# adaLN products and sums of squares in four 32-column tiles, and the residual's gate moved to the first group's head

## The chip, the cores and the metric

One core of a Trainium2 chip. The time is the device time of one execution in microseconds; of the kernel before there are three: 1978.23, 1971.2 and 1976.4, median 1976.4. Besides, one execution was taken by the hardware profiler; its span is 1971.9 us at a mean granted TensorE clock of 0.990. All durations of single instructions come from that execution.

## The reference

The kernel computes one layer of a bidirectional encoder for two requests ("groups" below: prompt and sample) that share all weights, each of 1024 tokens with 1024 channels, in float32. What the change touches is the frame around the two attention branches:

```
mod = silu(c) @ w_ada + b_ada                   # w_ada: 1024 x 3072, one c for each group
shift, scale, gate = split(mod, 3)
h = rms_norm(x, norm_g) * (1 + scale) + shift
proj = h @ w_in                                 # all of: qa, ka, va, za, qb, kb, vb, zb, ga, gb
oa = gqa_attention(qa, ka, va) * silu(za)       # branch A: 8 heads, RMS-normed, rotated
ob = headwise_norm(diff_attention(...)) * silu(zb)   # branch B
merged = sigmoid(ga) * (oa @ w_proj_a) + sigmoid(gb) * (ob @ w_proj_b)
y = x + gate * (merged @ w_out)
```

So `shift` and `scale` are needed before the first projection, while `gate` is needed only in the residual addition at the end of each group.

## The kernel before, in words

**Data.** Activations are kept transposed: channels on the 128 partitions, tokens along the free dimension, eight chunks of 128 channels, two halves of 512 tokens. For the large products each operand is split into a high and a low part in a rounded fp32 type, and a product is three matmuls (high x high, high x low, low x high). Weights come in pieces of 256 KB into small staging tiles ("st", three of them), from where ACT (L179) and POOL or DVE (L181) split them into a weight tile ("w", two of them). Large tiles ("u", 15 of 8 KB per partition) hold the activations, and in the head also the adaLN weights. PSUM has two large tiles ("s"), three of one bank ("f") and one for the attention's values ("a"). While no attention runs, `gbank()` deals out both s and f.

**Order.** The program text says which work belongs between which: `weave()` takes steps of several generators in turn, by shares. A scheduler then orders the instructions on each engine, with the attention's scores first; each engine works through its list in order and waits on semaphores. All DMAs that the change touches are issued by SP, one list, in order: a DMA that waits for its buffer holds up those behind it.

**The head of the first group.** `start()` (L339) loads c, the first half of x and eight 1 MB pieces of w_ada (L245 to L250: two column halves of shift and of scale, each in two row halves). `ada()` (L294) multiplies SiLU(c), 128 channels x 2 groups, as the stationary operand with 512 columns of w_ada: 4 chunks per piece, all added up in one PSUM row pair over 8 chunks (L300). These are plain fp32 products, which the trace shows as two passes each. `ada_end()` (L302) copies the 2 x 512 sums to SBUF (L306), transposes them by four small products (L309) and adds the bias (L313). For the RMS norm, ACT squares x (L256); for the first half of the tokens `added()` (L259) adds the eight chunks on DVE (L262 to L265) and `inv_rms()` (L268) sums over partitions by 128x1 products with a column of ones (L273), POOL takes the power -1/2 (L280), `spread()` (L283) brings the result to all partitions by products with the identity (L287) and an ACT copy (L289), and DVE and POOL multiply x by it (L356). For the second half there is no addition on DVE: `inv_rms()` gets all eight chunks, 32 products of 128x1 (64 passes). The shift and scale of that half stand in `start_late()` (L368), which `head()` (L1018) calls after the first six steps of the k/v projection of branch A and three of z: spread, then x times scale times statistics (L374, eight on DVE), shift and high part on ACT (L377, L378), low part on DVE (L379).

**Projections.** `proj_tt()` (matmuls at L514) makes q, k and v, a 128-token tile at a time; `z_gen()` (L692, matmuls at L703) makes the gate paths' inputs, which ACT evicts (L709) and SP stores in DRAM (L712).

**Attention.** 128 scores of branch A and 128 of branch B, half of each in the first group; a score is 128 query rows by 1024 keys for one head. For each: four matmuls (L734, L735), maximum on DVE (L736, L737), exponential on ACT (L738), a transposition on DVE (L771) and further by DMAs, split in two halves (L784 on ACT, L785 on DVE), and the matmuls with the values (L796, L797 for A, L836 for B). Between the scores PE runs "fill": the projections that the next stage needs. In the last stage of each group's attention the fill is made by `fill()` (L1141): z, gates' products and the merge.

**The residual's gate.** `gate_gen()` (L445) is the first thing in that fill of the first group. It loads the last third of w_ada in 16 pieces of 256 KB into the staging tiles (L451), multiplies each as above (L452, 32 passes), copies, transposes (L456, L459) and adds the bias.

Of the kernel before, what the change touches and what calls it, by code (L numbers as in the profile page):

```python
# [20 lines left out]
P = 128  # L21
T = 1024
D = 1024
# [45 lines left out]
WHOLE = (True, True)  # L69

# [20 lines left out]
def kernel(ctx: ExitStack, tc: tile.TileContext, t: dict):  # L91
# [81 lines left out]
    nc.vector.memset(nhalf, -0.5)  # L173

# [57 lines left out]
    cT = const.tile([P, NCH, 2], F32, name="cT")  # L232
# [26 lines left out]
    def added(sq):  # L259

        a, b = sq
        nc.vector.tensor_tensor(out=a[:, :2], in0=a[:, :2], in1=b[:, :2], op=ALU.add)  # L262
        nc.vector.tensor_tensor(out=a[:, 2:], in0=a[:, 2:], in1=b[:, 2:], op=ALU.add)
        nc.vector.tensor_tensor(out=a[:, :2], in0=a[:, :2], in1=a[:, 2:], op=ALU.add)
        nc.vector.tensor_tensor(out=a[:, 0], in0=a[:, 0], in1=a[:, 1], op=ALU.add)  # L265
        return [a[:, 0]]

    def inv_rms(sq):  # L268

        ps = gbank()  # L270
        for k in range(4):
            for i, x in enumerate(sq):
                nc.tensor.matmul(  # L273
                    ps[:, k : k + 1], x[:, k * P : (k + 1) * P], ones_c, start=(i == 0), stop=(i == len(sq) - 1)
                )
# [3 lines left out]
        nc.gpsimd.tensor_scalar(out=ss, in0=ss, scalar1=1.0 / D, scalar2=EPS, op0=ALU.mult, op1=ALU.add)  # L279
        nc.gpsimd.tensor_tensor(out=rs, in0=ss, in1=nhalf[:, :4], op=ALU.pow)  # L280
        return rs
# [12 lines left out]
    def ada(n, wt):  # L294
        hf, third, q = n // 4, n // 2 % 2, n % 2
        if q == 0:
            accs[n // 2] = gbank()[:2]
        acc = accs[n // 2]
        for c in range(4):
            nc.tensor.matmul(acc, cT[:, q * 4 + c], wt[:, c], start=(q == 0 and c == 0), stop=(q == 1 and c == 3))  # L300

    def ada_end(n):  # L302
        hf, third = n // 4, n // 2 % 2
        acc = accs[n // 2]
        row = halves2(ptile())[0][:2]
        nc.vector.tensor_copy(row, acc)  # L306
        ps = gbank()[:, :8].rearrange("p (c g) -> p c g", g=2)
        for c in range(4):
            nc.tensor.transpose(ps[:, c, :], row[:, c * P : (c + 1) * P], ident[:2, :2])  # L309
        cs = slice(hf * 4, hf * 4 + 4)  # L310
        mc = modc[:, third, cs, :]
        both = [P, 4, 2]
# [3 lines left out]
        if third:  # L316
            nc.vector.tensor_tensor(out=mc, in0=mc, in1=gcol[:, cs].unsqueeze(2).to_broadcast(both), op=ALU.mult)
# [21 lines left out]
    def start(ht):  # L339
        nc.scalar.activation(cT, ccol, AF.Silu)  # L340
# [9 lines left out]
        for n in range(8):  # L350
            ada(n, wts[n])
            if n == 3:
                rsb = spread(inv_rms(added(squares(xT[0]))))
# [3 lines left out]
            if n in (2, 4, 6, 7):  # L357
                ada_end(n if n == 7 else n - 1)
            if n == 4:
# [83 lines left out]


    def gate_gen():  # L445
        for half in range(2):
            acc = gbank()[:2]
            for k in range(NCH):
                st = spool.tile([P, 512], F32, tag="st", name=nm("st"))
                col = 2 * D + half * 512  # L450
                dma(st, w_ada[k * P : (k + 1) * P, col : col + 512])  # L451
                nc.tensor.matmul(acc, cT[:, k], st, start=(k == 0), stop=(k == NCH - 1))  # L452
                if k % 2:
                    yield 1
            row = rtile()[:2]
            nc.vector.tensor_copy(row, acc)  # L456
            ps = gbank()[:, :8].rearrange("p (c g) -> p c g", g=2)
            for c in range(4):
                nc.tensor.transpose(ps[:, c, :], row[:, c * P : (c + 1) * P], ident[:2, :2])  # L459
            cs = slice(half * 4, half * 4 + 4)  # L460
            nc.vector.tensor_tensor(
                out=gatec[:, cs], in0=ps, in1=bcol[:, 2, cs].unsqueeze(2).to_broadcast([P, 4, 2]), op=ALU.add
            )
# [554 lines left out]
    def head(g, st, zs, late):  # L1018
# [80 lines left out]
    states = [new_state(0), new_state(1)]  # L1099
    late = start(states[0]["ht"])  # L1100
    load_tables()
    for g in range(2):
# [38 lines left out]
        def fill():  # L1141
            if g == 0:
                yield from gate_gen()
# [68 lines left out]
```

## Time and profile before

| | us |
|---|---|
| times of three executions | 1978.23, 1971.2, 1976.4 |
| span of the profiled execution | 1971.9 |
| PE busy / DVE busy / ACT busy / POOL busy | 1901.8 / 1353.0 / 1012.0 / 680.9 |
| first product of the projections (L514) starts | 42.41 |
| second half's statistics spread (L287) | 66.09 |
| first product of a score (L734) starts | 140.7 |
| products of the residual's gate (L452) | 751.1 to 785.9 |

The profiled execution's own time stands by its span of 1971.9; it lies 4.5 below the median and within the three executions. In a row of the profile, "L703 PE MATMUL f<-u,w 128*128 128x512 f32 x2184 | 561.3, 395" means: 2184 instructions of line 703 on PE that write tile f from tiles u and w, 561.3 us of busy time, 395 ns for the mean one. Records of neighbouring matmuls overlap, so that the pace of a row of matmuls is read from the starts of two groups, not from the mean. "idle before" is the time that the engine stood just ahead of such instructions, and the name behind "<-" is what released it. One instruction of the program's text can stand as two in the trace: a plain fp32 matmul has two passes.

### The profile page before, as it was taken

The page shows a single profiled execution, that of the slowest core. Times are in us where ns is not written, and L with a number is a line of the kernel's source. Part 1 is how long each engine was busy: PE and PEld are TensorE (multiplying, and loading weights), DVE is VectorE, ACT ScalarE, POOL GpSimd, SP SyncE. Part 2 cuts the span into 40 slices and gives each one's busy share as a digit, 9 for nine tenths or more (in the row PEclk, how much of TensorE's full clock was granted, in tenths as well). Part 3 has the DMA queues.
Part 4 walks back from the last instruction along what each step waited for, and adds up shares of the span by engine and source line. Part 5 has one row for each costly group of instructions (what it writes and reads, how often), then busy time and mean ns, then how long its engine had stood idle before and what let it go on. Part 6 is the DMA issues. An engine that isn't in the chain of part 4 may idle for free. (4 is left out here: it accounts for less than half of the span.)

```text
span 1971.9 us, 30870 instructions
## 1 busy us (share of the span) xinstructions
PE 1901.8 (96%) x10466; PEld 1619.1 (82%) x10466; DVE 1353.0 (69%) x2165; ACT 1012.0 (51%) x1920; POOL 680.9 (35%) x958
## 2 busy tenths in 40 slices
PE   8999999999989999999999999999999999998999
PEld 3888888888878985778889788888888889776887
DVE  4658876786888577757465598768878766776641
ACT  4447655565655353464323576556666444447410
POOL 2363511442446251322235344114444426322210
PEclk9899999999999999999999999999999999999999
DMA  9125545556454345865641355555555334478431
GB/s 315 33 89 149 144 139 149 158 156 174 127 144 111 89 117 173 272 234 179 222 151 44 115 144 167 148 149 157 156 152 161 98 102 119 120 222 267 166 102 75
DMA packets 271614, 295.26 MB, mean 150 GB/s; under 512 B 37856, under 2 KB 220256, under 8 KB 271456
## 3 DMA queue, kind: packets, MB, share of 16 engines
q1 hardware_dynamic: 271456, 293.28, 50.1%
q8 instruction: 84, 1.38, 0.3%
q14 instruction: 74, 0.61, 0.1%
HBM read 133.72 MB, written 42.01 MB: 89 GB/s over the span
## 5 line engine op out<-in xcount | busy, mean ns | idle before, releaser
L703 PE MATMUL f<-u,w 128*128 128x512 f32 x2184 | 561.3, 395 | 3.0 <-ACT w L179 1.3
L514 PE MATMUL f<-w,u 128*128 128x256 f32 x3456 | 489.6, 286 | 5.2 <-ACT ev L709 2.7
L514 PEld LDWEIGHTS f<-w,u 128*128 128x128 f32 x3456 | 460.7, 192 | 26.8 <-ACT ev L709 3.7
L703 PEld LDWEIGHTS f<-u,w 128*128 128x128 f32 x2184 | 396.8, 189 | 78.1 <-ACT w L179 1.8
L181 POOL TENSOR_TENSOR w<-st,w 128x512 fp32r<-128x512 f32 x166 | 227.8, 1391 | 463.2 <-ACT w L179 412.9
L736 DVE TENSOR_REDUCE m<-s 128x1 f32<-128x1024 f32 x256 | 310.2, 1217 | 55.1 <-PE s L735 52.0
L771 DVE STREAM_TRANSPOSE p<-p 128x1024 f32<-128x1024 f32 x192 | 238.0, 1241 | 112.8 <-ACT p L738 110.2
L785 DVE TENSOR_TENSOR q<-q,hi 128x512 fp32r<-128x512 f32 x256 | 193.9, 774 | 47.9 <-ACT hi L784 46.4
L738 ACT ACTIVATE p<-s,m,rsB 128x1024 f32<-128x1024 f32 x128 | 154.0, 1204 | 135.0 <-DVE m L737 103.3
L738 ACT ACTIVATE p<-s,m,rsA 128x1024 f32<-128x1024 f32 x128 | 153.8, 1202 | 128.1 <-DMA q<-p 95.8
L735 PE MATMUL s<-u,sw 128*128 128x512 f32 x512 | 205.0, 401 | 0.0
L784 ACT ACTIVATE hi<-q 128x512 fp32r<-128x512 f32 x256 | 153.2, 624 | 78.2 <-DMA q<-p 50.2
L179 ACT ACTIVATE w<-st 128x512 fp32r<-128x512 f32 x196 | 114.2, 626 | 101.9 <-DMA st<-in_w_in_dram 46.6
L976 PE MATMUL f<-u,w 128*128 128x512 f32 x552 | 136.4, 400 | 11.3 <-ACT ev L709 4.1
L796 PE MATMUL a<-hi,u 128*128 128x256 f32 x512 | 132.0, 284 | 4.8 <-DVE oo L813 3.1
L976 PEld LDWEIGHTS f<-u,w 128*128 128x128 f32 x552 | 104.8, 192 | 35.3 <-DVE u L987 4.6
L836 PE MATMUL a<-q,u 128*128 128x256 f32 x512 | 125.9, 385 | 5.6 <-DMA q<-p 1.9
L797 PE MATMUL a<-q,u 128*128 128x256 f32 x512 | 129.8, 287 | 0.5 <-DVE q L785 0.4
L734 PE MATMUL s<-u 128*128 128x512 f32 x256 | 109.5, 428 | 7.9 <-ACT p L738 4.0
L734 PE MATMUL s<-u,u 128*128 128x512 f32 x256 | 103.3, 404 | 13.8 <-ACT p L738 9.0
L836 PEld LDWEIGHTS a<-q,u 128*128 128x128 f32 x512 | 95.9, 193 | 21.6 <-issue 2.9
L735 PEld LDWEIGHTS s<-u,sw 128*128 128x128 f32 x512 | 97.4, 190 | 15.5
(186 smaller groups left out, 2639.1 us busy)
## 6 DMA issues: line engine op xcount, KB each, us to landing
q<-p SPq DMA_DIRECT2D x768, 128.0 KB, 2.6
st<-in_w_in_dram SPq DMA_DIRECT2D x132, 256.0 KB, 3.0
zd<-ev SPq DMA_DIRECT2D x96, 256.0 KB, 2.2
sw<-u SPq DMA_DIRECT2D x256, 64.0 KB, 2.0
p<-zd SPq DMA_DIRECT2D x64, 256.0 KB, 3.8
u<-in_w_ada_dram SPq DMA_DIRECT2D x8, 1024.0 KB, 10.4
st<-in_w_in_dram SPq DMA_DIRECT2D x64, 128.0 KB, 2.7
st<-in_w_out_dram SPq DMA_DIRECT2D x32, 256.0 KB, 3.2
```

The lines of the kernel that those rows point to most:

```text
L181: e.tensor_tensor(out=wl, in0=st, in1=wh.bitcast(F32), op=ALU.subtract)
L514: nc.tensor.matmul(ps, lt[c][:, sl], w[:, c, wi, :], start=(k == 0), stop=(k == 23))
L703: nc.tensor.matmul(ps, w[:, c, wi, e * P : (e + 1) * P], rt[c], start=(k == 0), stop=(k == 23),)
L734: nc.tensor.matmul(s[:, sl], q, k[:, sl], start=True, stop=False)
L735: nc.tensor.matmul(s[:, sl], sw, k[:, sl], start=False, stop=True)
L736: nc.vector.tensor_reduce(out=m, in_=s, axis=AX.X, op=ALU.max, negate=True)
L738: nc.scalar.activation(pt.rearrange("p (j c a) -> p j c a", j=4, c=8), s.rearrange("p (c a j) -> p j c a", c=8, j=4), AF.Exp, scale=rs, bi ...
L771: nc.vector.transpose(pt, pt)
L784: nc.scalar.activation(th, tl.bitcast(F32), AF.Copy)
L785: nc.vector.tensor_tensor(out=tl, in0=tl.bitcast(F32), in1=th.bitcast(F32), op=ALU.subtract)
L836: nc.tensor.matmul(acc, u["v"][:, k], pT[:, k], start=(k == 0), stop=(k == 7))
L976: nc.tensor.matmul(ps, w[:, c, wi, d * P : (d + 1) * P], o[:, oi, :], start=(k == 0), stop=(k == 11))
```

## The change

- **Four products at once in 32-column tiles.** SiLU(c) is kept with 32 columns per chunk, 30 of them zero (`at`). `ada()` gives each of the four chunks of a piece its own 32 partitions of the PSUM bank (`quarter()`), that is, its own column tile of the array; a tile adds up two products only. `ada_end()` copies the whole 128 x 512 bank and contracts the four quarters by products with a 128 x 2 matrix (`two`), which takes the place of the transposes.
- **Sums of squares likewise.** `inv_rms()` multiplies 32 columns of -0.5 with the eight chunks of squares, four tiles with two products each, copies the bank, and contracts it by four 128x1 products; the factor -1/(16 D) makes up for the 32 equal rows and the -0.5. `added()` is gone.
- **Order in the head.** The pieces of w_ada come in the order shift, scale of the first column half, then of the second as before; the first half's statistics are made after the second piece, not the fourth; each pair of pieces is ended at once.
- **The residual's gate** is made in the first group's head by `gates_of_residual()`, right behind `late()`: four loads of 1 MB into u tiles, 16 products in tiles, two `ada_end()`. `gate_gen()` is gone, and with it its place in `fill()`.

```
+ADA = [(third, hf, q) for hf in range(2) for third in range(2) for q in range(2)]
+ADA += [(2, hf, q) for hf in range(2) for q in range(2)]
...
+    two = const.tile([P, 2], F32, name="two")
+    nc.vector.tensor_reduce(
+        out=two, in_=ident.rearrange("p (j r) -> p r j", j=4)[:, :2, :], axis=AX.X, op=ALU.add
+    )
...
-    def added(sq):
...
+    def quarter(ps, c):
+        return ps[32 * c : 32 * c + 32]
 
     def inv_rms(sq):
+        acc = gbank()
+        for i in range(2):
+            for c in range(4):
+                nc.tensor.matmul(quarter(acc, c), nhalf, sq[i][:, c], start=(i == 0), stop=(i == 1))
+        part = rtile()
+        nc.vector.tensor_copy(part, acc)
         ps = gbank()
         for k in range(4):
-            for i, x in enumerate(sq):
-                nc.tensor.matmul(
-                    ps[:, k : k + 1], x[:, k * P : (k + 1) * P], ones_c, start=(i == 0), stop=(i == len(sq) - 1)
-                )
+            nc.tensor.matmul(ps[:, k : k + 1], part[:, k * P : (k + 1) * P], ones_c, start=True, stop=True)
...
     def ada(n, wt):
-        hf, third, q = n // 4, n // 2 % 2, n % 2
+        third, hf, q = ADA[n]
         if q == 0:
-            accs[n // 2] = gbank()[:2]
-        acc = accs[n // 2]
+            accs[third, hf] = gbank()
+        acc = accs[third, hf]
         for c in range(4):
-            nc.tensor.matmul(acc, cT[:, q * 4 + c], wt[:, c], start=(q == 0 and c == 0), stop=(q == 1 and c == 3))
+            nc.tensor.matmul(quarter(acc, c), cT[:, q * 4 + c], wt[:, c], start=(q == 0), stop=(q == 1))
 
     def ada_end(n):
-        hf, third = n // 4, n // 2 % 2
-        acc = accs[n // 2]
-        row = halves2(ptile())[0][:2]
-        nc.vector.tensor_copy(row, acc)
+        third, hf, q = ADA[n]
+        row = rtile()
+        nc.vector.tensor_copy(row, accs[third, hf])
         ps = gbank()[:, :8].rearrange("p (c g) -> p c g", g=2)
         for c in range(4):
-            nc.tensor.transpose(ps[:, c, :], row[:, c * P : (c + 1) * P], ident[:2, :2])
+            nc.tensor.matmul(ps[:, c, :], row[:, c * P : (c + 1) * P], two, start=True, stop=True)
         cs = slice(hf * 4, hf * 4 + 4)
-        mc = modc[:, third, cs, :]
+        mc = modc[:, third, cs, :] if third < 2 else gatec[:, cs, :]
...
     def start(ht):
-        nc.scalar.activation(cT, ccol, AF.Silu)
+        nc.gpsimd.memset(cT, 0.0)
+        nc.scalar.activation(cT[:, :, :2], ccol, AF.Silu)
...
         for n in range(8):
             ada(n, wts[n])
-            if n == 3:
-                rsb = spread(inv_rms(added(squares(xT[0]))))
+            if n == 1:
+                rsb = spread(inv_rms(squares(xT[0])))
...
-            if n in (2, 4, 6, 7):
-                ada_end(n if n == 7 else n - 1)
-            if n == 4:
+            if n % 2:
+                ada_end(n)
+            if n == 3:
                 split_early(kva_w[0])
                 add_h(ht, 0, 0)
                 modulated(ht, 0, xT[0], range(4))
...
-        rs = inv_rms([q[:, c] for q in squares(xT[1]) for c in range(4)])
+        rs = inv_rms(squares(xT[1]))
...
+    def gates_of_residual():
+        for n in range(8, 12):
+            ada(n, load_ada(n))
+            if n % 2:
+                ada_end(n)
...
-    def gate_gen():
...
                 if i == 0:
                     late()
+                    gates_of_residual()
...
+    cT = mtile("at", [P, 256], bufs=1).rearrange("p (c m) -> p c m", c=NCH)
     late = start(states[0]["ht"])
...
         def fill():
-            if g == 0:
-                yield from gate_gen()
             yield from zs
```

In the kernel after, the lines that the prediction names have other numbers: the products of `ada()` stand at L304 (L300 before), the contraction at L312 (L309), the copy of the sums at L309 (L306), the products over the squares at L274 and L279 (L273), the spread at L291 (L287), the second half's L374 and L379 at L384 and L389.

More of the change, by code (lines that the diff above doesn't have):

```diff
@@ L231 @@
     gcol = const.tile([P, NCH], F32, name="gcol")
-    cT = const.tile([P, NCH, 2], F32, name="cT")
     modc = const.tile([P, 2, NCH, 2], F32, name="modc")
@@ L257, in squares @@
         return sq
-    def added(sq):
[L261 to L266, printed above, removed]
-    def inv_rms(sq):
+    def quarter(ps, c):
+        return ps[32 * c : 32 * c + 32]
+    def inv_rms(sq):
+        acc = gbank()
[4 more added lines that the diff above has]
+        nc.vector.tensor_copy(part, acc)
         ps = gbank()
         for k in range(4):
-            for i, x in enumerate(sq):
-                nc.tensor.matmul(
-                    ps[:, k : k + 1], x[:, k * P : (k + 1) * P], ones_c, start=(i == 0), stop=(i == len(sq) - 1)
-                )
+            nc.tensor.matmul(ps[:, k : k + 1], part[:, k * P : (k + 1) * P], ones_c, start=True, stop=True)
         ss = tiny.tile([P, 4], F32, tag="ss", name=nm("ss"))
@@ L278, in inv_rms @@
         nc.vector.tensor_copy(ss, ps[:, :4])
-        nc.gpsimd.tensor_scalar(out=ss, in0=ss, scalar1=1.0 / D, scalar2=EPS, op0=ALU.mult, op1=ALU.add)
+        nc.gpsimd.tensor_scalar(out=ss, in0=ss, scalar1=-1.0 / (16 * D), scalar2=EPS, op0=ALU.mult, op1=ALU.add)
         nc.gpsimd.tensor_tensor(out=rs, in0=ss, in1=nhalf[:, :4], op=ALU.pow)
@@ L294, in ada @@
     def ada(n, wt):
[L295 removed]
+        third, hf, q = ADA[n]
         if q == 0:
[L297 to L298 removed]
+            accs[third, hf] = gbank()
+        acc = accs[third, hf]
         for c in range(4):
[L300 removed]
+            nc.tensor.matmul(quarter(acc, c), cT[:, q * 4 + c], wt[:, c], start=(q == 0), stop=(q == 1))
     def ada_end(n):
[L303 to L306 removed]
+        third, hf, q = ADA[n]
+        row = rtile()
+        nc.vector.tensor_copy(row, accs[third, hf])
         ps = gbank()[:, :8].rearrange("p (c g) -> p c g", g=2)
         for c in range(4):
[L309 removed]
+            nc.tensor.matmul(ps[:, c, :], row[:, c * P : (c + 1) * P], two, start=True, stop=True)
         cs = slice(hf * 4, hf * 4 + 4)
[L311 removed]
+        mc = modc[:, third, cs, :] if third < 2 else gatec[:, cs, :]
         both = [P, 4, 2]
@@ L315, in ada_end @@
         )
-        if third:
+        if third == 1:
             nc.vector.tensor_tensor(out=mc, in0=mc, in1=gcol[:, cs].unsqueeze(2).to_broadcast(both), op=ALU.mult)
@@ L442, in load_tables_A @@
             st[name] = tab
-    def gate_gen():
[L446 to L463, printed above, removed]
     def ht_gen(g, ht):
```

## The prediction

> **What bounds the kernel now.** I read the page's busy table first, then its chain, then the busy time by stretches around the two places that the change touches: the head of the first group (0 to 80 us) and the last stage of its attention (740 to 860 us). Columns of the stretches: length, then busy time and count of PE, PEld, DVE, ACT and POOL, then granted clock, DMA share and GB/s.
>
> ```profile
> span 1971.9 us, 30870 instructions
> PE 1901.8 (96%) x10466; PEld 1619.1 (82%) x10466; DVE 1353.0 (69%) x2165; ACT 1012.0 (51%) x1920; POOL 680.9 (35%) x958
> PE 27%; DVE 5%; DMA 4%; SPq 3%; issue 2%; ACT 2%; POOL 1%; ACTq 0%; DVEq 0%; POOLq 0%
> ```
> ```profile
> 0.00:20.00 20.00, 12.42 (x26) 2.39 (x27) 4.85 (x9) 6.09 (x10) 0.69 (x6) 1.00 0.92 339
> 20.00:40.00 20.00, 20.00 (x59) 5.01 (x57) 12.18 (x20) 8.89 (x15) 7.15 (x6) 1.00 1.08 389
> 40.00:60.00 20.00, 20.00 (x110) 18.55 (x109) 10.25 (x28) 9.48 (x17) 4.94 (x4) 0.67 0.43 100
> 740.00:860.00 120.00, 110.29 (x462) 78.36 (x461) 84.78 (x130) 58.95 (x94) 27.68 (x36) 0.99 0.77 245
> ```
>
> PE is busy 96% of the span and leads the chain, so PE work taken out of a stage in which PE is the limit comes off the time, and PE work put where PE waits costs nothing. Two stretches are special. Up to 40 us the DMA engines are full (shares 0.92 and 1.08): PE looks busy there, but it works through the adaLN products as the weights land. From 40 to 60 us PE is busy throughout at a granted clock of 0.67 only. In the gate's stage PE idles 9.7 of 120 us.
>
> **The change part by part.** *The gate's products leave the attention.* The first fence below is the group of the gate's products and what PE waited for ahead of them; the second shows what eight products cost in a row.
>
> ```profile
> L452 PE MATMUL f<-st,cT x32: 591/592/592, 751.1 to 785.9; 128*2 128x512 f32 x32
>   DMA st<-in_w_ada_dram: 6.7, 10
>   issue: 4.3, 13
> ```
> ```profile
> 22.27 3.60 PE L300 MATMUL s<-u,cT 128*2 128x512 f32 x8
> 25.70 3.60 PE L300 MATMUL f<-u,cT 128*2 128x512 f32 x8
> ```
>
> The second group starts 3.43 us after the first, so one pass costs 0.43 us (a 592 ns record overlaps the next). 32 passes are 13.8 us. To that come the eight transposes (about 0.8) and some 2.5 of the 6.7 us in which PE's queues stood waiting for the gate's 256 KB loads. PE is 92% busy in this stage with the rest of its idle time small, so I count all of it: **-17**, between -13 (the bare passes less a little) and -21 (with all the load waits).
>
> *The head: what goes.* The head's timeline of before:
>
> ```profile
> 37.95 4.25 ACT L256 ACTIVATE q<-u 128x512 f32<-128x512 f32 x8
> 42.41 2.31 PE L514 MATMUL f<-w,u 128*128 128x256 f32 x12
> 40.87 1.28 PE L273 MATMUL f<-ones_c,q 128*128 128x1 f32 x10
> 47.23 8.09 PE L273 MATMUL f<-ones_c,q 128*128 128x1 f32 x50
> 55.18 4.19 PE L703 MATMUL s<-u,w 128*128 128x512 f32 x9
> 66.09 0.60 PE L287 MATMUL f<-ident,rs 128*128 128x128 f32 x4
> 67.54 13.26 SPq L712 DMA_DIRECT2D zd<-ev  x2
> 69.61 0.60 ACT L289 ACTIVATE ev<-f 128x512 f32<-128x512 f32 x1 [1.57 <-PE f L514]
> 70.25 5.93 DVE L374 SCALAR_TENSOR_TENSOR u<-u,modc,ev 128x512 f32<-128x512 f32 x8 [1.68 <-ACT ev L289]
> 61.09 2.23 PE L703 MATMUL s<-u,w 128*128 128x512 f32 x9
> 66.44 3.11 PE L514 MATMUL f<-w,u 128*128 128x256 f32 x24
> ```
> ```profile
> L379 DVE TENSOR_TENSOR u<-u,u x8: 676/679/693, 76.5 to 83.7; 128x512 fp32r<-128x512 f32 x8
> u<-in_w_ada_dram SPq DMA_DIRECT2D x8, 1024.0 KB, 10.4
> ```
>
> The first half's statistics come about 8 us sooner (no four DVE additions, and the spread no longer stands behind two more adaLN products), but that buys nothing: the first product of the input projection (42.41) follows the last adaLN weights and the second half of x, which the full DMA queues deliver no sooner. I expect it at 42.5 to 43 again. The 64 adaLN passes hide behind those loads at any spacing up to today's.
>
> What does count is the second half's sum of squares. Its 64 128x1 products (10 in 1.28 us, 50 in 8.09, four more) cost about 10 us between 40.9 and 55. In their place stand 8 products with 32 columns and four with one. One after another the 8 are 16 passes of 0.43 us, 6.9; four at once 1.7; but they can start as the squares finish (37.95 + 4.25), ahead of the projection. No row of before shows two column tiles at work: today's 32-column tile is always the first. I take a factor of 2 over one after another, because each of these fp32 products runs as two passes in order on one tile, so a neighbour can overlap only part. That gives 3.4 us, mostly behind the squares, and the spread of the second half at about 57 instead of 66.1: **-9**.
>
> *The head: what comes in.* In the built program's PE order, behind that spread, come the first two gate products, then the four contractions with the [128, 2] matrix, and only then the next products of z. Those contractions wait for a DVE copy of the gate's sums, and that copy stands on DVE behind all eight L374 and all eight L379 (the after's L384 and L389). From the rows these are 5.93 + 8 x 0.68 = 11.4 us of DVE work that starts about 1.6 us after the spread: until about 70.5. The first gate weights are late as well: on SP they stand behind the first z eviction, which in turn needs a finished z unit (about 58); at a landing of 10.4 us they arrive between 63 and 69. So from 57.6 to about 70.5 PE has only those gate products, where before it ran 72 products of z and of the k/v projection: **+13** of stall, gate products 8 and 9 in it. If the copy gets through sooner, say when the loads land at 65, it is +8. Gate products 10 and 11 follow among z products, 16 passes at the halved cost less what their weights' landing hides: **+2** (+0.5 to +7). Head: -9 + 13 + 2 = **+6**, from +1 to +13. In the built order the first attention score also stands behind 24 more z products (24 x 0.23 = 5.4 us); they are missing later, so this moves the first score without costing time.
>
> *The order of the first attention stage.* With the gate's pieces gone from the fill, the fill is dealt out otherwise. For nine scores of branch A (the 37th to the 45th) the built program has almost no projection products between the scores: 0.7 us, by the spacings above, where before has 35; by the 96th score the two have done the same sum again. The reason in the order is SP: the fourth piece of the next branch-B weight stands behind the transfers of later scores. Before, in that stretch and up to the 96th score:
>
> ```profile
> 337.00:389.00 52.00, 49.99 (x301) 43.94 (x300) 37.27 (x57) 32.31 (x63) 22.00 (x31) 1.00 0.57 160
> 389.00:660.00 271.00, 264.59 (x1555) 233.53 (x1554) 209.77 (x327) 152.67 (x305) 114.35 (x192) 0.99 0.50 139
> L736 DVE TENSOR_REDUCE m<-s x8: 1186/1216/1225, 345.2 to 385.3; 128x1 f32<-128x1024 f32 x8
> L785 DVE TENSOR_TENSOR q<-q,hi 128x512 fp32r<-128x512 f32 x17 | 12.2, 726 | 7.1 <-ACT hi L784 7.0
> L771 DVE STREAM_TRANSPOSE p<-p 128x1024 f32<-128x1024 f32 x9 | 11.2, 1242 | 7.0 <-ACT p L738 7.0
> L737 DVE TENSOR_TENSOR m<-m,rsA 128x1 f32<-128x1 f32 x8 | 1.4, 177 | 0.3
> L813 DVE TENSOR_TENSOR oo<-a,at 64x256 f32<-64x256 f32 x4 | 1.7, 418 | 0.1
> ```
>
> A score's own PE work is four products at 0.23 and eight at 0.13: 2.0 us. Its DVE work is 1.22 + 1.24 + 2 x 0.73 + 0.18 + 0.2 = 4.3, and with a little slack I take 4.5 us per score when nothing fills PE. Nine such scores leave PE idle 9 x 2.5 = 22.5 us. Before, PE idled 8.4 us in all from 337 to 660 us (2.0 and 6.4). The put-off 34 us of fill can take up nearly all the later idle time, not more. So 22.5 - 8.4 = 14, less about 1 for slack that other stretches give: **+13**. Bounds: the fastest pace of scores without much fill that before shows is branch B's in the second group,
>
> ```profile
> 1516.00:1544.00 28.00, 25.54 (x131) 20.85 (x130) 21.56 (x33) 12.82 (x25) 8.27 (x12) 1.00 0.57 157
> L736 DVE TENSOR_REDUCE m<-s x7: 1186/1217/1225, 1519.2 to 1542.6; 128x1 f32<-128x1024 f32 x7
> ```
>
> 6 steps in 23.4 us, 3.9 each; less some fill, 3.6. At 3.6 it is 9 x 1.6 - 8.4 = +6; at 5.2 (the chain with its transfers not overlapped) 9 x 3.2 - 8.4 = +20.
>
> *The second group.* Its order shifts by a few products only (up to 12 us of fill earlier, level again at score 192): **+2**, from -2 to +7, as the nearest stretch with idle PE there has 4.5 us of it:
>
> ```profile
> 1100.00:1140.00 40.00, 35.53 (x185) 29.65 (x184) 22.55 (x32) 26.66 (x42) 7.98 (x9) 0.96 0.46 126
> ```
>
> **Sum**: -17 + 6 + 13 + 2 = +4 on the span, 1971.9 to 1975.9. The profiled span is 4.5 below the median of 1976.4, so the median becomes about 1980.
>
> **The skill beside it.** The Trainium skill, "TensorEngine Tiling (Array Packing)", section Theoretical Speedup, gives up to 4x for an output dimension of 32 or less, and "TensorE: Matmul & The Clock Gate", Part 3, reports 2.38x for three column tiles with 512 moving columns. No run here shows it yet. By the full 4x the second half's squares and the gate in the head would be about 3 us shorter, which by my sum is 1977. Key Properties of the first page also says that a change of tiling mode drains the engine. The change puts such switches between full-width products; before has them too, and its rows show no gap of size there (22.27 + 3.60 runs on into 25.70), so I count nothing.
>
> **The rivals.**
> *Faster: the thin stretch is cheap.* If scores without fill run at 3.6 us and the put-off fill lands in idle time (+6), the copy gets through early (+1) and the gate's stage yields its waits too (-20), the sum is -13: 1963. For it: 9.7 us of idle PE in the gate's stage, and branch B's pace. Against it: branch A's DVE rows alone add up to 4.3.
> *Slower: the thin stretch is dear.* One mechanism, in the nine scores from the 37th on: without fill each takes 5 us or more, because max, exponential, transpose, transfer and the two halves follow one another; then the fill put off is paid nearly whole, +20. It decides from about 5 us per score. With the head at +10 and the gate at -14 the sum is +18 with the second group's +2: 1994. For it: in these rows DVE waits 7.0 us each for ACT at L771 and L785 within 52 us, that is, the chain isn't packed.
> *Slower: the tiles don't overlap.* The change then does not do what it says: 0.43 us per pass as now. The squares take 3.5 more, the gate's products in the head up to 7 more: +10 on my forecast, 1990.
> *Faster still: the order costs nothing* (no stall in the head, no thin stretch): -17 - 9 + 3 = -23, 1953.
>
> **How the numbers follow.** Forecast 0.40; cheap thin stretch 0.20; dear thin stretch 0.20; no overlap 0.15; no cost of order 0.05. 0.5%, about 9.9 us, is about what a measurement of this kernel can tell from no change: 1966.5 to 1986.3 counts as the same. Faster 0.25 (cheap stretch and no cost of order), same 0.40, slower 0.35. All terms at their low ends give -16 (1960), at their high ends +27 (2003); all at one end at once is unlikely. From 1963 to 1997 the range takes in the forecast, the cheap stretch's value, no overlap and the dear stretch.
>
> **What would show it.** Right: no gate products after 740 us and PE busy time in that stage down by some 14; PE idle for 8 us or more between about 57 and 71 us, ended by the DVE copy at L309; PE busy about half in a stretch of nine A scores near 340 to 400 us, at about 4.5 us per score; passes of L304 0.2 us apart where weights are there. Wrong: the spread of the second half at 66 us still (then the squares cost what the sums cost); passes 0.43 apart (no overlap) or 0.11 (full overlap); PE full from 340 to 400 us, by which the +13 falls and the time is near 1967.

## The result, and the profile after

The changed kernel takes 2030.5 us (median of four, 2025.7 to 2037.1) against 1974.0 for the kernel before (median of four): a ratio of 1.029, 95% interval 1.0267 to 1.0313, 56.6 us slower. The forecast was 1980, and its range ended at 1997. The profiled execution has a span of 2025.9 us, 54.0 more than before's.

The page of the changed kernel, its first lines and its chain:

```profile
span 2025.9 us, 30873 instructions
PE 1900.4 (94%) x10466; PEld 1626.0 (80%) x10466; DVE 1343.4 (66%) x2164; ACT 1019.8 (50%) x1924; POOL 676.1 (33%) x959
PE 15%; DMA 2%; DVE 2%; ACT 1%; issue 1%; SPq 0%; POOL 0%; ACTq 0%; DVEq 0%; POOLq 0%
```

PE is busy as long as before (1900.4 against 1901.8 us) with as many passes (10466 in both), of which some now run four at a time. So all 54 us are time in which PE stood, and part of the busy time is work at a lower clock (mean 0.971 against 0.990). Busy time by stretches of the changed kernel (columns as in the prediction):

```profile
0.00:20.00 20.00, 11.44 (x48) 3.64 (x48) 2.08 (x8) 6.11 (x10) 1.70 (x9) 1.00 0.92 328
20.00:40.00 20.00, 12.65 (x68) 5.05 (x70) 14.40 (x19) 9.38 (x16) 7.27 (x5) 0.71 1.06 371
40.00:60.00 20.00, 17.68 (x79) 12.02 (x74) 11.25 (x30) 9.66 (x19) 5.29 (x5) 0.69 0.58 129
60.00:80.00 20.00, 8.65 (x51) 4.71 (x49) 13.09 (x26) 12.30 (x22) 4.25 (x8) 0.73 0.63 224
100.00:120.00 20.00, 11.96 (x95) 11.18 (x93) 13.13 (x41) 7.13 (x26) 13.04 (x24) 0.84 0.12 39
```

From 20 to 40 us, where before's PE was busy throughout at full clock, PE is busy 12.65 us at 0.71. From 60 to 80 us it stands 11 us, from 100 to 120 us 8 us.

To see where the time is lost I cut each kernel at four points that every version has: the start of the maximum of the 1st, 97th, 145th and 256th score. The maximum's line tells them; these are its rows from the start to the 97th and to the 145th score, of before and after:

```profile
L736 DVE TENSOR_REDUCE m<-s x97: 1184/1224/1226, 141.9 to 675.2; 128x1 f32<-128x1024 f32 x97
L736 DVE TENSOR_REDUCE m<-s x145: 1173/1224/1226, 141.9 to 1183.1; 128x1 f32<-128x1024 f32 x145
```
```profile
L725 DVE TENSOR_REDUCE m<-s x97: 1175/1225/1226, 169.9 to 715.2; 128x1 f32<-128x1024 f32 x97
L725 DVE TENSOR_REDUCE m<-s x145: 1175/1220/1226, 169.9 to 1225.5; 128x1 f32<-128x1024 f32 x145
```

The second pair is of after. The first section is the head, the second most of the first group's attention, the third holds the gate's stage (the first group's last 32 scores), the first group's end, the second group's head and its first 16 scores, the fourth the rest of the second group's attention, the fifth the tail. All kernels of this study, in us of one profiled execution each, and as difference from before (single executions of one kernel differ by up to 13 us in all, so differences of a few us in one cell should not be leaned on):

| kernel | head | scores 1-97 | 97-145 | 145-256 | tail | span |
|---|---|---|---|---|---|---|
| before | 141.9 | 533.3 | 507.8 | 603.3 | 185.5 | 1971.9 |
| after | +28.0 | +12.0 | +2.4 | +5.6 | +6.1 | 2025.9 |
| e1 gate back in the last stage | +4.2 | +15.0 | +4.6 | +6.9 | +7.5 | 2010.2 |
| e2 only the gate moved | +23.6 | +6.8 | -3.4 | +4.8 | -0.4 | 2003.3 |
| e3 before, no gate | -0.1 | -2.6 | +0.6 | +1.3 | -1.2 | 1970.0 |
| e4 after, no gate | +10.3 | +11.1 | -1.7 | +7.4 | -3.7 | 1995.4 |
| e5 before, a second spread | +12.3 | +12.4 | +8.8 | -1.3 | +0.3 | 2004.3 |
| e6 gate at the head's end | +19.8 | +6.6 | +6.9 | +11.2 | +7.3 | 2023.7 |
| e7 old squares in the second half | +28.1 | +5.8 | -1.0 | +1.2 | -0.9 | 2005.2 |
| e8 adaLN products three times | +22.9 | +11.2 | -2.5 | +5.9 | -1.4 | 2007.9 |
| f1 after, banks as before | +18.5 | +1.2 | -7.1 | +3.4 | -0.4 | 1987.6 |
| f2 e1, banks as before | -1.6 | +5.3 | +3.6 | +2.9 | +0.3 | 1982.5 |
| f3 before, counter begins at 1 | +10.0 | +14.5 | +5.1 | +3.2 | -0.6 | 2004.2 |
| f4 before, counter +2 late | +1.0 | -0.5 | +2.1 | +4.7 | +4.7 | 1984.0 |
| g1 f1, gate at the head's end | +10.5 | +11.3 | -5.2 | +7.2 | -1.3 | 1994.4 |
| g2 f1, gate's weights early | +8.6 | +4.8 | -4.7 | +4.5 | -1.0 | 1984.2 |

### The profile page after: what moved, and what is told of

It is laid out like the page before. It is cut to its first block, busy times and chain, and to the rows that moved or that the text cites. A ratio compares the mean times of both kernels' runs of the same rounds, so it can differ in the third digit from the quotient of the medians.

```text
span 2025.9 us, 30873 instructions
## 1 busy us (share of the span) xinstructions
PE 1900.4 (94%) x10466; PEld 1626.0 (80%) x10466; DVE 1343.4 (66%) x2164; ACT 1019.8 (50%) x1924; POOL 676.1 (33%) x959
## 5 line engine op out<-in xcount | busy, mean ns | idle before, releaser
L774 DVE TENSOR_TENSOR q<-q,hi 128x512 fp32r<-128x512 f32 x256 | 186.4, 747 | 59.4 <-ACT hi L773 55.8
L965 PE MATMUL f<-u,w 128*128 128x512 f32 x576 | 146.1, 406 | 12.3 <-DVE u L976 8.0
L786 PE MATMUL a<-q,u 128*128 128x256 f32 x512 | 133.2, 291 | 3.5 <-DVE q L774 1.7
L825 PE MATMUL a<-q,u 128*128 128x256 f32 x512 | 127.2, 389 | 9.0 <-DVE m L726 3.6
L558 ACT ACTIVATE u<-f 64x256 fp32r<-64x256 f32 (+1 forms) x202 | 73.2, 364 | 81.3 <-DVE u L559 56.6
```

The costliest lines, as they stand in the source:

```text
L774: nc.vector.tensor_tensor(out=tl, in0=tl.bitcast(F32), in1=th.bitcast(F32), op=ALU.subtract)
L825: nc.tensor.matmul(acc, u["v"][:, k], pT[:, k], start=(k == 0), stop=(k == 7))
L965: nc.tensor.matmul(ps, w[:, c, wi, d * P : (d + 1) * P], o[:, oi, :], start=(k == 0), stop=(k == 11))
```

## The experiments

**First round: is it the tiles or the gate?**

e1 keeps the tiles and puts the gate's old products back:

```
-                    gates_of_residual()
...
+            if g == 0:
+                yield from gate_gen()
```

> The tiles and the new order of the head stay, the residual's gate is computed in the last attention stage again, by the old products. Theory A (the move of the gate costs the time: the stall in the head, the put-off fill, and a last stage that its products had only covered): the first score starts within 8 us of before's 141.9, no thin stretch, 1966 to 1982. Theory B (the tiles cost it: PE waits between weights, its clock falls, and the projections start 8 us later): the first score stays over 15 us late and the time is 1990 or more.

Measured: 2012.7 us, ratio 1.0192 (1.0162 to 1.0222), first score at 146.1. The first score agrees with theory A, the time with theory B's figure, so neither theory holds as a whole. The head is nearly as fast as before's, yet 34 us are lost behind it, most of them in stages that the edit doesn't touch.

e2 moves the gate alone, in the form of products that before has:

```
+                    gates_of_residual()   # acc = gbank()[:2], 16 products with cT, transposes
...
-                yield from gate_gen()
```

> The kernel before with only the residual's gate moved to the head, in the old form of products (no tiles, old sums of squares). Theory A: most of the loss, 2010 to 2040. Theory B: within 10 us of before, 1965 to 1985.

Measured: 2002.3 us, 1.0142 (1.0115 to 1.017), between the two expectations. Most of its loss is in the head (+23.6). After this round it looked as if the move cost the head and the tiles cost elsewhere: the move alone loses 27 us, the tiles alone 37.

e3 and e4 leave the gate's products out, of before and of after:

```
-                yield from gate_gen()                 (e3)
-                    gates_of_residual()               (e4)
+   nc.vector.tensor_copy(gatec, bcol[:, 2].unsqueeze(2).to_broadcast([P, NCH, 2]))
```

> The kernel before without the gate's products, loads and transposes at all (the gate is its bias alone, so the product with w_ada's last third is left out). By the prediction's term, the stage gets 13 to 21 us shorter: 1953 to 1961. If the products only covered waits of the attention's chain: within 5 us of before, 1968 to 1979.

Measured: 1971.3 us, 0.998 (0.9964 to 0.9995), about 4 us less, as expected if the products only covered waits. The stretch from 740 to 860 us of e3 shows PE's busy time:

```profile
740.00:860.00 120.00, 105.47 (x445) 84.90 (x444) 82.04 (x126) 69.85 (x100) 27.12 (x34) 0.90 0.67 201
```

and the groups of its PE in that stretch, with the idle time ahead of them, show what the gate's products had covered:

```profile
L955 PE MATMUL f<-u,w 128*128 128x512 f32 x108 | 29.1, 417 | 5.2 <-DVE row L925 3.7 <-DVE u L966 1.3 <-DVE u L927 0.2
L713 PE MATMUL s<-u 128*128 128x512 f32 x34 | 15.2, 448 | 4.6 <-ACT p L717 4.5
L920 PE MATMUL f<-ident,ssB 128*128 128x128 f32 x16 | 3.4, 349 | 2.5 <-DVE ssB L839 2.5
```

Before's PE stood 9.7 us of this stretch at a clock of 0.99; without the gate it stands 14.5 us, for the exponential (L713) and for DVE's norm of the gated branch (L955, L920), and the clock falls to 0.90. Over the 105 us of busy time the lower clock is another 9 to 10 us, an estimate from the two granted clocks.

> The changed kernel without the gate's products at all (the gate is its bias alone). By theory A the head loses its 17 us of stall and the time falls by 15 to 25, to 2005 to 2015; the rest stays with the order of the first stage and the last stage. By theory B it falls by less than 8, 2022 or more.

Measured: 1994.5 us, 1.0105 (1.008 to 1.0131), 36 us less than after: more than either theory. Of the 30.5 us between the profiled spans the head gives 17.7; the rest comes from later sections, for which neither theory has a cause.

**Second round: the parts of the head, and a neutral change.**

```
e5:  rs0 = inv_rms(added(squares(xT[0])));  rsb = spread(rs0);  rsb = spread(rs0)     (before)
e6:  gates_of_residual() behind the weave of the head's projections                  (after)
e7:  rs = inv_rms_old([q[:, c] for q in squares(xT[1]) for c in range(4)])            (after)
e8:  for n < 8 each adaLN product twice more, into a bank of its own                 (after)
```

> The kernel before with the first half's statistics spread twice (one more row of four products and an ACT copy, the first result thrown away): under 1 us of work at 30 us. Theory O (the loss in the attention stages is the scheduler's new dealing-out of fill, which any small shift in the head sets off): the first score within 3 us of before, and then a gain or loss of 5 us or more by the 97th score. Theory S (the order follows from what the change does): the order of the first stage stays, and the time is within 3 us of before.

Measured: 2004.6 us, 1.014 (1.0102 to 1.0179). Under 1 us of work costs 31. Theory O is right that a small shift in the head loses time in the attention (+12.4 by the 97th score), but it expected the first score within 3 us of before, and that came 12.3 late. What the trigger is came out only in the next round.

> The changed kernel with the gate's products put behind all of the head's projections in the program's text. Theory A (the stall of 17 us behind the second half's spread is due to the place: weights late on SP, sums copied behind the second half's chain on DVE): no PE wait for w_ada between 60 and 85 us, first score 12 to 20 us sooner than in the changed kernel (150 to 158), 2005 to 2018. Rival (the gate's 4 MB and products cost the head their time wherever they are): first score at 165 or later, 2024 or more.

Measured: 2020.5 us, 1.023 (1.0193 to 1.0267); first score at 161.7. Both lie between the two expectations. In the trace PE has no wait for the weights there any more. But 48 more z products than in before (168 against 120) and 24 more of k and v stand ahead of the first score, so that the head's figure doesn't tell the two apart; g1 does it again.

> The changed kernel with the second half's sum of squares in the old form (32 products of 128x1 that may stand between projections). If the tile form is what starts the projections late (12 passes and a copy ahead of them at a low clock), they start at 43 to 45 us, not 50.6, but the spread comes later than 64.2; the first score within 4 us of the changed kernel. If the projections still start at 49 or later, it is ACT's order of the squares and not their products.

Measured: 2007.4 us, 1.0172 (1.0141 to 1.0202). The projections start at 43.0 us, as expected, and the first score stays (170.0). The old form's price is in these rows of e7, the 128x1 products and the second half's spread:

```profile
43.00 2.48 PE L517 MATMUL f<-w,u 128*128 128x256 f32 x10
46.56 11.94 PE L291 MATMUL s<-ones_c,q 128*128 128x1 f32 x56
70.02 0.60 PE L305 MATMUL f<-ident,rs 128*128 128x128 f32 x4
```

and its stretch from 40 to 60 us:

```profile
40.00:60.00 20.00, 20.00 (x92) 19.32 (x89) 10.14 (x26) 8.97 (x16) 4.32 (x4) 0.50 0.57 129
```

56 passes of one column take 11.94 us, at a granted clock of 0.50 in that stretch; what starts 7.5 us sooner spreads 6 us later. In total e7 is 23 us faster than after, all of it behind the head; the third round has a reason for that, too.

> The changed kernel with every product of the head's first eight adaLN pieces made three times (two of them thrown away). If the low clock after the waits for weights is a cost by itself: the granted clock of 20 to 60 us rises from 0.70 to over 0.85 and the first score comes 3 us sooner or more. If the clock costs little there: first score 0 to 6 us later, by the added passes.

Measured: 2013.0 us, 1.02 (1.0165 to 1.0236). The stretches of e8:

```profile
20.00:40.00 20.00, 16.36 (x132) 6.10 (x136) 14.51 (x20) 9.54 (x17) 7.42 (x5) 0.91 1.07 372
40.00:60.00 20.00, 19.14 (x141) 13.25 (x132) 11.15 (x30) 10.19 (x22) 4.43 (x4) 1.00 0.55 118
```

The clock rises as expected from 0.71 to 0.91 and from 0.69 to 1.00, and the first score comes 5.1 us sooner. How much of the 5 is the clock stays open: this kernel asks for eight banks more, which shifts the order, too.

**Third round: the banks.** e5's second spread does one thing besides its work: it asks for a PSUM bank. While no attention runs, the kernel deals these out by a counter:

```
        turn[0] += 1
        if alone[0] and turn[0] % 5 in (0, 2):
            return sbank()[:, :512]
        return fbank()
```

Before asks 12 times in the adaLN part and the statistics and four more times for the gate. The change asks 18 times, all in the head. Six more requests are one place further in a cycle of five for what follows the gate in the head; behind the last stage, where before asks its last four times, the two kernels stand two places apart. While attention runs, every request gets an f bank wherever the counter stands, so the attention can feel a shift in the head only through the order that it brings about. The next four kernels move nothing but the counter:

```
f1 (after): turn[0] += 3 at the end of start(), += 1 behind the gate, += 4 in the first group's fill()
f2 (e1):    turn[0] += 3 at the end of start()
f3 (before): turn = [1]
f4 (before): turn[0] += 2 behind gate_gen()
```

> The changed kernel, with the counter that deals PSUM banks between the s and the f tiles set forward at three places (end of the adaLN part +3, behind the gate +1, at the last stage's fill +4), so that every later product gets the kind of bank that it had before. No work is added or taken away. Theory P (what is lost behind the head comes from the banks' dealing having shifted: the change asks 18 times for a bank where before asks 16 times, 6 of them more in the head): from score 1 to 97 within 5 us of before, from score 145 to the end within 5 us, the head still 15 to 28 us late: 1988 to 2004. Theory C (the change's own work and waits set off the new order): within 8 us of the changed kernel, 2020 or more.

Measured: 1995.1 us, 1.0113 (1.0077 to 1.0149): 35 of the 57 us are gone with a counter. Scores 1 to 97 take +1.2, the rest from 145 on +3.0, the head +18.5: theory P in each part.

> The run with the tiles in the head and the gate back in the last stage, now with the counter set forward by 3 at the end of the adaLN part. Theory P: all of its loss of 37 us goes; the head keeps a gain of 0 to 6 us, 1965 to 1977. Theory C: 2000 or more.

Measured: 1984.3 us, 1.0052 (1.0033 to 1.0071). 28 of e1's 37 us go and the head is 1.6 us shorter than before's, but 12 us stay behind it; theory P's range was missed by 7. What is left isn't the counter at these places, and stays open.

> The kernel before with the counter started at 1, not 0; nothing else, no work added. Theory P: as the run with the second spread, which also asks for one bank more, +20 to +35: 1993 to 2010. Theory C: within 4 us of before.

Measured: 2006.8 us, 1.0166 (1.0131 to 1.02), as theory P expects. No work is added. The shift by one explains details of after's head as well. These are the z products ahead of the first score, of before and of f3, and a wait in f3:

```profile
L703 PE MATMUL f<-u,w 128*128 128x512 f32 x72 | 18.2, 397 | 0.0
L703 PE MATMUL s<-u,w 128*128 128x512 f32 x48 | 14.1, 443 | 0.0
```
```profile
L703 PE MATMUL f<-u,w 128*128 128x512 f32 x72 | 20.1, 425 | 0.0
L703 PE MATMUL s<-u,w 128*128 128x512 f32 x72 | 18.0, 397 | 0.0
102.62 0.47 PE L567 MATMUL f<-ident,row 128*128 128x128 f32 x1 [6.60 <-POOL row L556]
```

f3 has 24 z products more ahead of its first score (72 + 72 against 72 + 48), and so have e5 and after; f1 has 120 like before. In runs of 24 they stand in s, f, f, f, s in before, f1 and f2, and in f, s, f, s, f, s in after, e5 and f3. The wait of 6.60 us for POOL at the same products is 6.64 in e5 and 6.55 in after, and f1 has none there.

> The kernel before with the counter set forward by 2 behind the gate's products in the last stage, so that only what follows gets other banks: in total as the changed kernel. Theory P: nothing before the 97th score; from score 145 to the end 8 to 18 us more, as in the three kernels with that total: 1982 to 1994. Theory C: within 4 us of before.

Measured: 1979.3 us, 1.0029 (1.0011 to 1.0046); from score 145 on +9.4 in the profiled execution, whose span lies above the median; in the median +5. That execution is the slowest of ten, and the median misses P's range, which began at 1982: the direction is P's, the size is smaller.

The stretch in which the prediction saw a lack of fill shows the same thing. Busy time of f1 from 337 to 389 us:

```profile
337.00:389.00 52.00, 51.40 (x301) 45.28 (x300) 36.24 (x50) 28.78 (x55) 17.56 (x22) 0.98 0.59 147
```

of f3 in the same stretch:

```profile
337.00:389.00 52.00, 36.04 (x180) 29.39 (x180) 44.13 (x63) 33.22 (x61) 11.27 (x13) 0.90 0.58 157
```

and of after from 353 to 396 us, with the maxima of its ten scores there:

```profile
353.00:396.00 43.00, 31.24 (x150) 24.90 (x148) 38.36 (x53) 26.53 (x48) 4.49 (x4) 0.88 0.62 147
```
```profile
L725 DVE TENSOR_REDUCE m<-s x10: 1202/1221/1225, 355.6 to 395.6; 128x1 f32<-128x1024 f32 x10
```

f1, which has all of the change's work, has no thin stretch (PE 51.4 of 52 us); f3, which has none of it, has one (36.0 of 52), like after (31.2 of 43).

e7 bears theory P out without having been made for it. It asks once less than after, 17 times in the head, so that its counter stands a full turn of five beyond before's behind the head, and one place, not two, behind the last stage: scores 1 to 97 cost +5.8, not +12.0, and from 145 on +0.3, not +11.7. How the scheduler gets from other banks in the head to a thin stretch 200 us later was not followed.

**Fourth round: the gate in the head.** f1 and f2 differ only in the gate (its place, and with it the form of its products and loads): 20.1 us in the head. Here are f1's products in that place and what PE waited for:

```profile
64.44 0.60 PE L291 MATMUL f<-ident,rs 128*128 128x128 f32 x4
71.94 1.94 PE L304 MATMUL f<-u,at 128*32 128x512 f32 x8 [6.91 <-DMA u<-in_w_ada_dram]
74.69 1.94 PE L304 MATMUL f<-u,at 128*32 128x512 f32 x8 [0.82 <-DMA u<-in_w_ada_dram]
80.72 1.87 PE L312 MATMUL s<-two,row 128*128 128x2 f32 x8 [4.09 <-DVE row L309]
```

g1 has f1's banks and the gate behind the head's projections; g2 is f1 with the four loads asked for at the end of the adaLN part:

```
g1:  gates_of_residual() behind the weave; turn[0] += 1 behind it
g2:  gate_w.extend(load_ada(n) for n in range(8, 12)) at the end of start(); ada(n, gate_w[n - 8])
```

> The changed kernel with the banks dealt as before at the same three places, and the gate's products behind all of the head's projections in the text: in the built order its weights are asked for behind three z evictions and its 16 products stand among the last z products ahead of the first score. If the gate's 20 us in the head are the wait of that place (weights and DVE copy late, nothing else for PE): the head falls from 160.4 to 142 to 150 and the time to 1972 to 1985. If they are its passes, switches and 4 MB wherever they are: head 155 or later, 1990 or more.

Measured: 1992.7 us, 1.0102 (1.0071 to 1.0134); head 152.4, in the middle of the gap between the two expectations: 8 of the 20 us go with the place. The time lies where the rival has it, but only half of that is the head's doing: scores 1 to 97 cost +11.3 here, although the banks behind the head are dealt as before. So the counter is not the only thing that can upset the order of the attention.

> The changed kernel with the banks dealt as before and the gate's four loads asked for at the end of the adaLN part, ahead of the first z eviction on SP; its products stay where they are. If the stall is the weights' lateness: the 6.9 and 0.8 us of waiting for w_ada go, the wait for the DVE copy stays or grows by up to as much (the copy stands behind the second half's chain, which ends at about 80 us). By the DVE queue alone the head stays within 3 us of 160.4; by the weights alone it falls by 6 to 9. I expect the first, 157 to 161, as the copy's place on DVE ends last.

Measured: 1986.3 us, 1.0073 (1.0044 to 1.0101); head 150.5. My expectation of 157 to 161 was wrong: 9.9 us go. With the weights there early the copy is done early as well, ahead of the second half's chain, and PE doesn't wait for it:

```profile
65.67 2.78 PE L305 MATMUL f<-u,at 128*32 128x512 f32 x24
71.65 1.07 PE L305 MATMUL f<-u,at 128*32 128x512 f32 x8
```

Half of the gate's 20 us in the head are thus the lateness of its weights; the other half must be its passes, the contractions and what they push back, but it was not taken apart further. No version beats the kernel before; the one without any gate (e3) is the only one below it.

## Why the prediction was wrong, point by point

The terms were -17, +6, +13 and +2. With the 24 early z products counted where the prediction counts them (5.5 us, out of the head and into scores 1 to 97), after's sections give +2.4, +22.5, +17.5 and +11.7: 54 us instead of 4. Three steps failed: the gate's products were priced as if PE limited their stage, the head was taken as nearly free, and the dealing of the banks, 38 of the 54 us, has no term of its own.

**The gate's products leave the last stage: -17 predicted.** This is the term that is furthest off. In after the section 97 to 145 is 2.4 us longer; with the banks as before, f1 against f2, it is 10.6 shorter; without the gate at all (e3 against before) it is 0.6 longer. So the leaving is worth something between nothing and 10.6 us, by the order that goes with it, and never the 17. I took PE's 92% as a bound and counted the passes whole. e3's rows show where they went: without the filler PE stands 4.8 us longer in this stage, for the exponential and DVE's norm, and its lower clock takes another 9 to 10, together about the 13.8 us of the passes. I called the stage's PE idle time "small" and did not ask what PE waits for once the filler is gone.

**The head, what goes: -9 predicted, -1.9 measured.** The spread of the second half came at 64.18, not at 57. The head of after, its squares, the first projections, the spread and the gate:

```profile
43.52 1.52 ACT L326 ACTIVATE u<-u,modc 128x512 f32<-128x512 f32 x2 [2.83 <-DVE modc L320]
44.95 1.13 ACT L262 ACTIVATE q<-u 128x512 f32<-128x512 f32 x2
45.62 2.43 PE L274 MATMUL s<-q,nhalf 128*32 128x512 f32 x4 [1.54 <-ACT q L262]
48.83 1.87 PE L279 MATMUL f<-ones_c,row 128*128 128x1 f32 x8 [0.78 <-DVE row L276]
50.56 3.97 PE L503 MATMUL f<-w,u 128*128 128x256 f32 x17
64.18 0.60 PE L291 MATMUL s<-ident,rs 128*128 128x128 f32 x4
71.57 1.94 PE L304 MATMUL f<-u,at 128*32 128x512 f32 x8 [6.79 <-DMA u<-in_w_ada_dram]
80.49 1.87 PE L312 MATMUL s<-two,row 128*128 128x2 f32 x8 [4.08 <-DVE row L309]
82.22 4.50 PE L692 MATMUL s<-u,w 128*128 128x512 f32 x10
120.85 0.47 PE L556 MATMUL f<-ident,row 128*128 128x128 f32 x1 [6.55 <-POOL row L545]
```

The step that failed is "I expect it at 42.5 to 43 again". The 128x1 products of before could stand between projections; the tile products all come ahead of them in PE's order and wait for ACT's last two squares, which start at 44.95 because ACT has the shift of the first half ahead of them and stood 2.83 us for its input (L326). So the projections start at 50.56, 8.1 us late, and eat the gain. e7 shows it from the other side (43.0 with the old form).

**The head, what comes in: +13 stall predicted.** Right in its mechanism: PE waited 6.79 us for the weights and 4.08 for the DVE copy, both named. From the spread's end (64.78) to the next z product (82.22) it is 17.4 us, not 13; the granted clock of 0.73 from 60 to 80 us, at which the contractions and the gate's passes run, is part of that. Products 10 and 11 take 1.07 us each, the +2. Of the 28.0 us by which the first score is late, f1 and f2 give 20.1 to the gate and -1.6 to the tiles; the other 9.5 go with the counter (after against f1), and among them is the wait of 6.55 us in the last row. The prediction saw the 24 z products ahead of the first score in the built order but not where they came from, and it didn't have the wait. Its range for the head was added up wrongly as well: its own ends give -0.5 to +11, not +1 to +13.

**The thin stretch: +13 predicted.** It is there, at the place and the pace forecast: ten scores 40.0 us from the first to the last, 4.4 us each, PE 73% busy. With the 24 early z products taken back, scores 1 to 97 cost 12.0 + 5.5 = 17.5. The stretch itself was read from the built program's order, so that its place and pace are no luck; but the cause isn't what I gave. I put it down to SP's order as a consequence of the gate's leaving; f1 and f3 show that it comes and goes with the shift in the dealing of banks, and in f1 the gate has left, too.

**The second group: +2 predicted, +11.7 measured.** f1 has +3.0 there. The three kernels whose edits leave the counter two places further by the end (after, e1, e6) have +11.7, +14.4 and +18.5 from score 145 on; f4, with that shift alone, has +9.4 (in its slowest execution); all others have at most 5.9.

Summed up, of the 54 us in the profiled spans 38.3 go with the counter (after against f1). The other 15.7 are f1 against before: the tiles alone, with the banks as before, cost 10.6 (f2 against before), none of it in the head and its cause open; the gate in the head adds 20.1 there, takes 10.6 off the later stage, and lowers scores 1 to 97 by 4.1 (f1 against f2). My rivals had none of the counter: I took a shift of order seen in the built program as a property of the change. (The cheap rival's -13 also left out the second group's +2.)

**The overlap of the tiles: factor 2 assumed.** 24 passes took 10.46 us in before (from 30.15 on) and 2.78 in g2, where the weights lay ready, both at a granted clock of 1.00:

```profile
30.15 10.46 PE L300 MATMUL f<-u,cT 128*2 128x512 f32 x24
```

That is a factor of 3.8, or 0.12 us a pass, the prediction's own sign of full overlap. The reason that I gave for 2, two passes in order on one tile, does not hold. The "up to 4x" of the Trainium skill, "TensorEngine Tiling (Array Packing)", section Theoretical Speedup, agrees with these rows; the 2.38x of the Trainium skill, "TensorE: Matmul & The Clock Gate", Part 3, is for three tiles, which no run here has. The better overlap bought nothing in the first 40 us, where the weights set the pace. The rows that the prediction cites for switches between tile shapes (22.27, 25.70) hold two groups of one shape; before's rows next to them do hold a switch (128x1 products from 21.29 for 1.05 us, then the adaLN products at 22.27), and no gap shows there either.

## What to carry to other kernels

Before you price a change that adds a request to a pool or rotating counter, or drops one, ask which later requests get another buffer; shift the counter alone and measure that first. A term for work taken out of a nearly full engine needs the answer to what that engine would wait for instead; if the chain beside it is as long, the work was cover and is worth little. Comparing two variants by sections between points that both have shows at once which losses lie where the edit can't reach.

## What the runs showed of the hardware that was not expected

Products that became four times faster, while their operands arrived no sooner, went with a lower clock. From 20 to 40 us before's slow products kept PE busy 20.00 us at a granted clock of 1.00; the fast ones kept it busy 12.65 us at 0.71, and with each product made three times (e8) it was 16.36 us at 0.91. That a wait of some microseconds halves the clock is what the Trainium skill, "TensorE: Matmul & The Clock Gate", Part 1, states; the rows are means over 20 us and fit it. The next 20 us show less: after ran at 0.69 there and e8 at 1.00, but before had only 0.67.

A PE that the profile shows as busy can run at half clock. From 40 to 60 us before was busy for 20.00 us at 0.67, and e7 for 20.00 us at 0.50; both have a long row of 128x1 fp32 products there. In such rows a pass took 0.16 us in before (50 in 8.09 us) and 0.21 in e7 (56 in 11.94 us), for one column of result; ten in before at a clock of 1.00 took 1.28 us, 0.13 each. Whether the small products cause the low clock or only meet it was not tested.
